# The second adaLN pass moved from attention to the paired merge-gate products, in halves of a block

## The chip, the cores and the metric

The kernel runs on one core of one Trainium2 chip. The metric is the device time of one execution in microseconds (us). Three runs of the kernel before took 3650.43, 3655.60 and 3663.57 us; the median is 3655.6 us. A measurement of this kernel can tell about 0.3% from no change.

## What is computed

The program is one step of a diffusion backbone of two layers over 128 prompt tokens and 1024 sample tokens, with a model width of 1024. In each layer adaLN makes a shift, a scale and a gate for every feature out of a conditioning vector, for the prompt and for the sample apart. The three go into the norm ahead of the layer and into the residual at its end. The gates `merge_g` of the merge are 3072 of the columns of the layer's input projection.

```python
def adaln_projection(x, cond, p):
    mod = jax.nn.silu(cond) @ p['w_ada'] + p['b_ada']
    shift, scale, gate = jnp.split(mod[:, None, :], 3, axis=-1)
    h = rms_norm(x, p['norm_g']) * (1.0 + scale) + shift
    return split_columns(h @ p['w_in']), gate

def merge_branches(o_a, o_b, o_c, merge_g, p):
    s_a, s_b, s_c = jnp.split(jax.nn.sigmoid(merge_g), N_BRANCH, axis=-1)
    m = s_a * (o_a @ p['w_pa']) + s_b * (o_b @ p['w_pb']) + s_c * (o_c @ p['w_pc'])
    return m @ p['w_o']

x = x + res_gate * merge_branches(o_a, o_b, o_c, merge_g, p)
```

`w_ada` has 1024 rows and 3072 columns in a layer. The kernel takes its columns in six blocks of 512: 0 and 1 are the shift, 2 and 3 the scale, 4 and 5 the gate.

## The kernel before

A layer runs in three parts: `front` (input projection, short convolutions, DeltaNet), `attention` and `mix` (merge gates, branch projections, merge, output projection, residual, next norm). Activations are held with features on the partitions. In the parts that use single-pass TensorE operands, a value is split into a rounded high part and a low part, and each product is three matmuls.

**Order.** In `front` and `mix` the code is written as streams (generators) that yield one instruction at a time. `Flow` (line 183) holds modelled costs and delays, and always emits the instruction that could start first by its model, with a small preference by rank (`RK`, line 264). Streams wait for each other by named events. All instructions that go through `Flow` have line 98 in the profile. `attn_all` (line 1241) emits directly, and its instructions have line 95. Each engine works off its own queue in that order.

**Attention.** `attn_all` goes through groups: a head and half of the sample tokens, nine blocks of keys each, a slot for each block, and two groups for the prompt at the end. In a slot `st` multiplies keys by queries (three matmuls), ACT takes the exponential into `P`, and POOL adds `P` up in `acc`. Three slots later the group's products with V follow (`po`), and the sums (`sm`). Twelve row maxima of the group after next are computed meanwhile: PE writes `s` into one of two places in PSUM (pool `pa`), and DVE reduces it to `mx` (`s1`, line 1311).

**adaLN.** Blocks 0 to 3 of layer 0 are computed at the start of the program (`s_ad`). The others are computed by `s_adv` (line 601) in attention: blocks 4 and 5 of layer 0 and 0 to 3 of layer 1 in layer 0, and blocks 4 and 5 of layer 1 in layer 1. For a block it loads eight tiles of 128 features by 512 columns (256 KB) in turn into two places. For each tile and each of the two conditioning vectors one instruction multiplies by a scalar of the partition and adds to an accumulator `ada` of 512 columns, on ACT for the first tile and on DVE for the rest. Then PE sums the accumulator over partitions with a matrix of ones (`adr`), ACT copies it (`ads`), PE turns rows into columns (`adc`), and DVE writes `mod` (`mod_put`, line 533). The table `AD` (line 767) spreads these steps evenly over the slots.

**Merge gates.** At the start of `mix` the stream `s_sg` (line 2113) computes the gates for three weight tiles directly, then for ten pairs of weight tiles with seven products in place of eight (a product is two halves of 288 tokens, 12 matmuls each). The order of the seven is in `SB`. `s_sh` (line 2006) makes the sums of activations, `s_sw` (line 2031) loads the weights of a pair (`ss`, `ws`), makes four sums of them on DVE, and splits each of the seven operands on ACT and POOL into its place (`sl0` to `sl4` and two in a tile `wh_sl`). `s_se` evicts each half product on DVE or ACT out of one of six places in PSUM, and `s_sx` takes tanh on ACT and stores the gates through SP. Event `sw{n}_{i}` says that operand i of pair n is in its place, `sp{n}_{i}` that its product has ended.

## Time and profile before

| what | value |
|---|---|
| median of 3 runs | 3655.6 us (3650.43 to 3663.57) |
| the profiled execution | 3672.03 us, its span 3670.1 us |
| busy: PE, DVE, POOL, ACT | 94%, 63%, 42%, 32% |
| attention with adaLN, layer 0 | 1006 to 1253 us, mean granted clock 0.78 |
| products of the pairs, layer 0 | 1397 to 1620 us, mean granted clock 1.00 |
| attention with adaLN, layer 1 | 2820 to 3039 us, mean granted clock 0.89 |

The profile shows one execution. Busy shares are means over stages with different limits, so a change in one stage is read from that stage. The granted clock is TensorE's, as a share of its full speed of 2.4 GHz; the other level is 1.2 GHz, and a mean between them says how long each held. Of the name in a row, the part to the left of the arrow is what an instruction writes and to the right what it reads. A matmul of plain 32-bit operands shows as two records.

### The profile page before, as it was taken

To read this page: it belongs to the slowest core of one execution; us is meant where nothing else is said; L and a number is where in the kernel's file an instruction comes from. 1 tells how busy PE (TensorE), PEld (TensorE's weight loads), DVE (VectorE), ACT (ScalarE), POOL (GpSimd) and SP (SyncE) were. 2 spreads that over 40 slices of the span, in tenths; PEclk is the share of its full clock that TensorE was granted. 3 is DMA by queue.
4 is the path that set the end of the run, shared out by engine and by line. 5 is a ranking of instruction groups with operands and counts; after the bars stand their busy time and mean duration, and the time that the engine had idled before them with its cause. 6 is when DMAs were issued, how large, how long until landed. Compare 5 with 4: busy or idle time off the path is not lost. (4 is left out here: it accounts for less than half of the span.)

```text
span 3670.1 us, 65225 instructions
## 1 busy us (share of the span) xinstructions
PE 3460.2 (94%) x24622; PEld 2934.9 (80%) x24622; DVE 2319.4 (63%) x4956; ACT 1189.8 (32%) x2543; POOL 1526.5 (42%) x1534
## 2 busy tenths in 40 slices
PE   7999999998978999999999999999998899999998
PEld 4988777778844589999999877777887557999998
DVE  4477676755577756447565777777456764743756
ACT  4432222224232333332344232122243333333234
POOL 3165556432244545422322645654313654542241
PEclk9999889999977899999999999999999989999999
DMA  5232212225633323347422233123265322333842
GB/s 185 93 109 74 58 49 74 69 57 167 192 92 97 76 69 99 105 130 240 147 100 92 88 79 80 46 55 81 82 202 154 89 56 62 99 99 115 252 148 84
DMA packets 372409, 389.62 MB, mean 106 GB/s; under 512 B 161280, under 2 KB 293056, under 8 KB 371712
## 3 DMA queue, kind: packets, MB, share of 16 engines
q1 hardware_dynamic: 372096, 385.46, 35.8%
q8 instruction: 195, 3.19, 0.4%
q14 instruction: 118, 0.97, 0.1%
HBM read 264.54 MB, written 120.72 MB: 105 GB/s over the span
## 5 line engine op out<-in xcount | busy, mean ns | idle before, releaser
L98 PE MATMUL ip<-h,wh_wi 128*128 128x384 f32 x5328 | 1165.2, 357 | 2.3 <-DVE gb L98 1.1
L98 PEld LDWEIGHTS ip<-h,wh_wi 128*128 128x128 f32 x5328 | 930.6, 194 | 55.3 <-issue 17.2
L95 POOL TENSOR_TENSOR acc<-acc,P 128x512 f32<-128x512 f32 x224 | 301.4, 1346 | 215.2 <-ACT P L95 203.9
L98 POOL TENSOR_TENSOR tmp<-M,X 128x2 f32<-128x2 f32 (+30 forms) x310 | 216.3, 698 | 278.1 <-DVE X L98 260.1
L95 DVE TENSOR_REDUCE mx<-s 128x1 f32<-128x384 f32 (+1 forms) x400 | 209.7, 542 | 183.3 <-PE s L95 177.1
L95 ACT ACTIVATE P<-st 128x512 f32<-128x512 f32 x292 | 173.6, 597 | 396.1 <-PE st L95 359.7
L95 PE MATMUL st<-q,K 97*128 97x512 f32 (+1 forms) x912 | 295.1, 440 | 0.0
L98 POOL TENSOR_TENSOR mU<-mU,mt 128x384 f32<-128x384 f32 x96 | 112.7, 1175 | 266.5 <-DVE mt L98 266.5
L95 PEld LDWEIGHTS st<-q,K 97*128 97x128 f32 x912 | 184.0, 214 | 42.7 <-issue 16.5
L98 POOL TENSOR_TENSOR wh_wi<-wri,wh_wi 128x512 fp32r<-128x512 f32 x112 | 153.1, 1377 | 156.0 <-ACT wh_wi L98 153.7
L98 PE MATMUL pp<-ob,wp 128*128 128x384 f32 x1152 | 210.4, 341 | 5.9 <-ACT ob L98 3.9
L98 PEld LDWEIGHTS pp<-ob,wp 128*128 128x128 f32 x1152 | 201.7, 190 | 14.0 <-ACT ob L98 6.9
L95 PE MATMUL s<-K,q 96*128 96x384 f32 (+1 forms) x400 | 150.3, 397 | 66.1 <-DVE mx L95 54.0
L98 POOL TENSOR_TENSOR sl<-ss,sl 128x512 fp32r<-128x512 f32 x100 | 140.0, 1403 | 155.4 <-ACT sl L98 143.7
L98 PE MATMUL wop<-h,wh_wo 128*128 128x384 f32 x1152 | 203.4, 336 | 0.5 <-DVE wh_wo L98 0.5
L98 DVE TENSOR_REDUCE X<-tmp 128x1 f32<-128x2 f32 (+30 forms) x620 | 184.6, 319 | 29.8 <-POOL tmp L98 22.0
L98 PEld LDWEIGHTS wop<-h,wh_wo 128*128 128x128 f32 x1152 | 199.6, 188 | 2.2 <-DVE wh_wo L98 1.1
L98 PE MATMUL sg<-T,sl 128*128 128x288 f32 x1440 | 194.4, 295 | 0.6 <-POOL sl L98 0.6
L98 PEld LDWEIGHTS sg<-T,sl 128*128 128x128 f32 x1440 | 192.0, 188 | 0.9 <-POOL sl L98 0.8
L98 ACT ACTIVATE VT<-pv,sst 128x64 f32<-128x64 f32 x256 | 66.4, 310 | 370.9 <-DVE scr L98 354.4
L95 PEld LDWEIGHTS s<-K,q 96*128 96x128 f32 x400 | 86.1, 215 | 119.9 <-DVE mx L95 91.5
L98 DVE TENSOR_TENSOR tmp<-M,X 128x2 f32<-128x2 f32 (+30 forms) x310 | 164.7, 531 | 19.4 <-POOL M L98 13.5
(343 smaller groups left out, 6376.5 us busy)
## 6 DMA issues: line engine op xcount, KB each, us to landing
wri<-in_w_in SPq DMA_DIRECT2D x160, 256.0 KB, 3.4
mt<-mD SPq DMA_DIRECT2D x144, 192.0 KB, 2.6
wada<-in_w_ada SPq DMA_DIRECT2D x64, 256.0 KB, 2.9
or<-oD SPq DMA_DIRECT2D x72, 192.0 KB, 3.6
wrp<-in_w_p SPq DMA_DIRECT2D x48, 256.0 KB, 3.6
mD<-C SPq DMA_DIRECT2D x80, 144.0 KB, 1.8
mD<-cu SPq DMA_DIRECT2D x80, 144.0 KB, 1.8
ss<-in_w_in SPq DMA_DIRECT2D x40, 256.0 KB, 3.6
```

The source lines that it names most:

```text
L95: return real(*a, **kw)
L98: op.f = lambda: real(*a, **kw)
```

## The change

`s_adv` becomes a stream of the first part of `mix`, with rank 4, and starts when the sums of activations have ended (`sT`). It works on half a block at a time: tiles of 128 features by 256 columns (128 KB) in two places, one accumulator of two times 256 columns. The sum over partitions is made by four matmuls for a half, with the accumulator as the stationary operand and one column of ones as the moving one, so that the result stands in columns at once; the matmuls with rows, their copy on ACT and the turning fall away. The rest of attention is the same.

Operand 3 of a pair takes the place of operand 0 (`slot[0]`), and `sl3` falls away. Its split is now the last of the pair and waits for product 0 of the same pair; the split of operand 0 waits for product 3 of the pair before. The accumulator's buffer serves `s_sh` as a scratch tile first.

```diff
--- before.py
+++ after.py
@@ -262,7 +262,7 @@
 
 
 RK = dict(ad=1, mk=0, mkb=5, xl=0, adl=1, w=2, ip=9, ev=1, cv=4, la=0, ga=7, gb=6, gv=4, gz=4, gc=3, gd=4, w2=2, lb=3, ln=0, ln1=1,
-          mw=2, mg=4, mp=5, em=1, ep=0, ob=3, xo=4, ms=1, mk1=3, ad1=4, adl1=1, mo=3, sh=3, sw=2, sg=5, se=0, sx=1)
+          mw=2, mg=4, mp=5, em=1, ep=0, ob=3, xo=4, ms=1, mk1=3, ad1=4, adl1=1, mo=3, sh=3, sw=2, sg=5, se=0, sx=1, adv=4)
 
 
 class Kern:
@@ -598,54 +598,43 @@
                 yield from cols
                 cols = None
 
-    def s_adv(self, blocks):
-
-
-        cs = yield from self.cond(blocks[0][0])
-        items = [(l, b, k) for l, b in blocks for k in range(KC)]
+    def s_adv(self, l):
+
+
+        yield Wait("sT")
+        cs = yield from self.cond(l)
+        blocks = [(l, b) for b in (4, 5)] + [(k, b) for k in range(l + 1, min(l + 2, L)) for b in range(4)]
+        items = [(k, b, x, kc) for k, b in blocks for x in range(2) for kc in range(KC)]
         w = {}
 
         def load(i):
             if i < len(items):
-                l, b, k = items[i]
-                w[i] = self.pt.tile([128, 512], F32, tag="wad", bufs=2, name=f"wada{l}_{b}_{k}")
-                yield self.ld(w[i], self.A["w_ada"][l, b][:, k * 512:k * 512 + 512])
-
-        def sums(l, b, acc):
-            rows = self.PA(f"adr{l}_{b}")
+                k, b, x, kc = items[i]
+                w[i] = self.al(self.pt, [128, 256], F32, "wad", 2, f"wada{k}_{b}_{x}_{kc}")
+                yield self.ld(w[i], self.A["w_ada"][k, b][:, kc * 512 + x * 256:kc * 512 + x * 256 + 256])
+
+        yield from load(0)
+        for i, (k, b, x, kc) in enumerate(items):
+            yield from load(i + 1)
+            if kc == 0:
+                if b == 0 and x == 0:
+                    self.mod_tiles(k)
+                acc = self.al(self.pt, [128, self.HC], F32, "wac", 1, f"ada{k}_{b}_{x}")[:, 0:512].rearrange("p (c x) -> p c x", c=2)
             for c in range(2):
-                yield self.mm(rows[c * 32:c * 32 + 32, :], self.ones[:, 0:32], acc[:, c], tile_position=(0, c * 32))
-            sr = self.pt.tile([128, 512], F32, tag="sr", name=f"ads{l}_{b}")
-            yield self.cp("a", sr[0:64], rows[0:64])
-            yield
-            yield
-            ps = self.PA(f"adc{l}_{b}")
-            for i in range(4):
-                yield self.mm(ps[:, i * 2:i * 2 + 2], sr[0:64, i * 128:i * 128 + 128], self.ident[0:64, 0:33:32])
-            yield from self.mod_put(l, b, ps)
-
-        for i in range(2):
-            yield from load(i)
-        todo = iter(())
-        for i, (l, b, k) in enumerate(items):
-            if k == 0:
-                if b == 0:
-                    self.mod_tiles(l)
-                acc = self.pt.tile([128, 2, 512], F32, tag="wah", bufs=2, name=f"ada{l}_{b}")
-            for c in range(2):
-                s = cs[:, k, c:c + 1]
-                if k == 0:
+                s = cs[:, kc, c:c + 1]
+                if kc == 0:
                     yield self.nc.scalar.activation(out=acc[:, c], in_=w[i], func=AF.Copy, scale=s)
                 else:
                     yield self.stt(acc[:, c], w[i], s, acc[:, c], ALU.mult, ALU.add)
-            yield from load(i + 2)
-
-            if k:
-                next(todo, None)
-                next(todo, None)
-            if k == KC - 1:
-                todo = sums(l, b, acc)
-        yield from todo
+            if kc == KC - 1:
+                if x == 0:
+                    ps = self.al(self.ppa, [128, 512], F32, "pa", 2, f"adc{k}_{b}")
+                for j in range(2):
+                    for c in range(2):
+                        o = (2 * x + j) * 2 + c
+                        yield self.mm(ps[:, o:o + 1], acc[:, c, j * 128:j * 128 + 128], self.ones[:, 0:1])
+                if x:
+                    yield from self.mod_put(k, b, ps)
 
 
     def rstd(self, acc, n, nm, buf, psum, res=None):
...
-    AD = (14, 24)
...
-        ad = [(l, b) for b in (4, 5)] + [(k, b) for k in range(l + 1, min(l + 2, L)) for b in range(4)]
-        ga = self.s_adv(ad)
-        n0, n1, m = *self.AD, len(ad) * 31 + 12
-        for i in range(m):
-            add(n0 + i * (NS - n1 - n0) // m, next, ga, None)
-        add(NS - n1 + 1, lambda: self.now(ga))
...
@@ -1971,7 +1950,8 @@
         R = lambda S: {n: dict(rank=RK[n], gen=g) for n, g in S.items()}
         X = {}
         with self.pool("pS", 1) as self.pt, self.pool("ppS", 1, space=PSUM) as self.ppm:
-            S = R(dict(sh=self.s_sh(l, X), sw=self.s_sw(l, X), sg=self.s_sg(l, X), se=self.s_se(l, X), sx=self.s_sx(l, X)))
+            S = R(dict(sh=self.s_sh(l, X), sw=self.s_sw(l, X), sg=self.s_sg(l, X), se=self.s_se(l, X), sx=self.s_sx(l, X),
+                       adv=self.s_adv(l)))
             fl.run(S)
         with self.pool("pm", 1) as self.pt, self.pool("ppm", 1, space=PSUM) as self.ppm:
             X["o"] = {}
@@ -2012,7 +1992,8 @@
 
         cf = cu.rearrange("p a x -> p (a x)")
         a, b = cf[:, N1], cf[:, N2]
-        c, e = (self.pt.tile([128, 1024], F32, tag=f"sl{i}", name=f"tq{l}_{i}")[:, N1] for i in (3, 4))
+        c = self.pt.tile([128, 1024], F32, tag="sl4", name=f"tq{l}")[:, N1]
+        e = self.al(self.pt, [128, self.HC], F32, "wac", 1, f"te{l}")
         for k in range(4):
             whole = lambda g, o, k, n: self.tt(g, o, f(h[:, k, 0, n]), f(h[:, k, 1, n]), ALU.add)
             yield whole("v", a, k, N2)
@@ -2033,7 +2014,9 @@
 
         def place(n):
             for i in range(len(slot), n):
-                slot.append(self.pt.tile([128, 1024], F32R, tag=f"sl{i}", name=f"sl{l}_{i}").rearrange("p (s x) -> p s x", s=2))
+
+                slot.append(slot[0] if i == 3 else self.pt.tile([128, 1024], F32R, tag=f"sl{i}", name=f"sl{l}_{i}").rearrange(
+                    "p (s x) -> p s x", s=2))
 
         place(3)
         tile_ = lambda x: self.A["w_in"][l, MT_MG + self.BR[x // 8] * 8 + x % 8]
@@ -2056,7 +2039,7 @@
             def free(i):
 
                 if not first:
-                    yield Wait(f"sp{n - 1}_{i}")
+                    yield Wait(f"sp{n - 1}_{3 if i == 0 else i}")
 
             yield self.ld(a11, w1[:, 0:512])
             r1, r2 = (self.al(self.pev, [128, 512], F32, "wr", 2, f"ws{l}_{n}_{x}") for x in range(2))
@@ -2079,9 +2062,6 @@
             yield from free(2)
             yield from split(2, s2)
             yield Set(f"sw{n}_2")
-            yield from free(3)
-            yield from split(3, s1)
-            yield Set(f"sw{n}_3")
             yield from free(4)
             yield from split(4, a11)
             yield Set(f"sw{n}_4")
@@ -2095,6 +2075,9 @@
             yield from free(6)
             yield from split(6, r2)
             yield Set(f"sw{n}_6")
+            yield Wait(f"sp{n}_0")
+            yield from split(3, s1)
+            yield Set(f"sw{n}_3")
         X["w"] = {}
         X["w"][23] = self.wh(f"mg{l}_23")
         yield from self.split_w(X["w"][23], 1024, tile_(23), f"m{l}_23", "p")
```

In DVE's queue in attention of layer 0 the maxima `mx` of group 4 stand between sums of adaLN (`ada`) before:

```order
L95 TENSOR_SCALAR nm_3_10601<-mx_3_10232 128x4
L95 TENSOR_REDUCE mx_4_10466<-s_4_0_10603 128x1
L95 TENSOR_REDUCE mx_4_10466<-s_4_1_10606 128x1
L95 SCALAR_TENSOR_TENSOR ada_4_10567<-wada_4_2_10580,cs_10547,ada_4_10567 128x512
L95 TENSOR_REDUCE mx_4_10466<-s_4_2_10624 128x1
L95 TENSOR_REDUCE mx_4_10466<-s_4_3_10639 128x1
L95 SCALAR_TENSOR_TENSOR ada_4_10567<-wada_4_3_10613,cs_10547,ada_4_10567 128x512
L95 RECIPROCAL sm_0_10505<-sm_0_10505 128x256
L95 TENSOR_REDUCE mx_4_10466<-s_4_4_10669 128x1
```

and now:

```order
L95 TENSOR_SCALAR nm_3_10588<-mx_3_10232 128x4
L95 TENSOR_REDUCE mx_4_10466<-s_4_0_10590 128x1
L95 TENSOR_REDUCE mx_4_10466<-s_4_1_10593 128x1
L95 TENSOR_REDUCE mx_4_10466<-s_4_2_10608 128x1
L95 TENSOR_REDUCE mx_4_10466<-s_4_3_10622 128x1
L95 RECIPROCAL sm_0_10505<-sm_0_10505 128x256
L95 TENSOR_REDUCE mx_4_10466<-s_4_4_10649 128x1
```

The sums between the maxima are gone.

In DVE's queue at the products of pair 2 of layer 0 stood the evictions (`cu`, `C`, from the products `sg_pair_operand_half`) and the weight sums `ss` of the pair to come:

```order
L98 TENSOR_TENSOR cu_13002<-sg_1_6_1_13578,cu_13002 128x288
L98 TENSOR_TENSOR C_2_0_13658<-sg_2_1_0_13633,cu_13002 128x288
L98 TENSOR_TENSOR C_2_1_13666<-sg_2_1_1_13648,cu_13002 128x288
L98 TENSOR_TENSOR ss_13229<-ws_3_0_13608,ws_3_1_13609 128x512
L98 TENSOR_TENSOR ss_13229<-ss_13229 128x512
L98 TENSOR_TENSOR cu_13002<-sg_2_2_0_13665,cu_13002 128x288
L98 TENSOR_TENSOR cu_13002<-sg_2_2_1_13686,cu_13002 128x288
L98 TENSOR_TENSOR cu_13002<-sg_2_3_0_13701,cu_13002 128x288
```

Now the sums of the second half of block 4 stand there, two for each load `wada`, and the weight sums come later:

```order
L98 TENSOR_TENSOR cu_12731<-sg_1_6_1_13357,cu_12731 128x288
L98 SCALAR_TENSOR_TENSOR ada_4_1_13279<-wada_4_1_3_13347,cs_13056,ada_4_1_13279 128x256 x2
L98 SCALAR_TENSOR_TENSOR ada_4_1_13279<-wada_4_1_4_13360,cs_13056,ada_4_1_13279 128x256 x2
L98 SCALAR_TENSOR_TENSOR ada_4_1_13279<-wada_4_1_5_13394,cs_13056,ada_4_1_13279 128x256 x2
L98 SCALAR_TENSOR_TENSOR ada_4_1_13279<-wada_4_1_6_13406,cs_13056,ada_4_1_13279 128x256 x2
L98 TENSOR_TENSOR C_2_0_13457<-sg_2_1_0_13416,cu_12731 128x288
L98 TENSOR_TENSOR C_2_1_13463<-sg_2_1_1_13440,cu_12731 128x288
L98 TENSOR_TENSOR cu_12731<-sg_2_2_0_13462,cu_12731 128x288
L98 TENSOR_TENSOR cu_12731<-sg_2_2_1_13481,cu_12731 128x288
L98 SCALAR_TENSOR_TENSOR ada_4_1_13279<-wada_4_1_7_13443,cs_13056,ada_4_1_13279 128x256 x2
L98 TENSOR_TENSOR cu_12731<-sg_2_3_0_13495,cu_12731 128x288
L98 SCALAR_TENSOR_TENSOR mod_158<-adc_4_13265,sm_122 128x8
```

Four loads' sums lie between the last eviction of pair 1 and the first one of pair 2 on DVE, and the last load's directly behind the eviction of half 2_2_1.

In PE's queue at the same place the products followed one another:

```order
L98 MATMUL sg_2_1_1_13648<-h,sl_1_12996 128x288 x12
L98 MATMUL sg_2_2_0_13665<-T_1_12999,sl_2_12997 128x288 x12
L98 MATMUL sg_2_2_1_13686<-T_1_12999,sl_2_12997 128x288 x12
L98 MATMUL sg_2_3_0_13701<-T_0_12998,sl_3_13327 128x288 x12
L98 MATMUL sg_2_3_1_13719<-T_0_12998,sl_3_13327 128x288 x12
```

and now the sums over partitions (`adc`) stand among them:

```order
L98 MATMUL sg_2_1_1_13440<-h,sl_1_12725 128x288 x12
L98 MATMUL sg_2_2_0_13462<-T_1_12728,sl_2_12726 128x288 x12
L98 MATMUL sg_2_2_1_13481<-T_1_12728,sl_2_12726 128x288 x12
L98 MATMUL sg_2_3_0_13495<-T_0_12727,sl_0_12724 128x288 x10
L98 MATMUL adc_4_13265<-cst,ada_4_1_13279 128x1
L98 MATMUL sg_2_3_0_13495<-T_0_12727,sl_0_12724 128x288 x2
L98 MATMUL sg_2_3_1_13513<-T_0_12727,sl_0_12724 128x288
L98 MATMUL adc_4_13265<-cst,ada_4_1_13279 128x1 x3
L98 MATMUL sg_2_3_1_13513<-T_0_12727,sl_0_12724 128x288 x11
```

The first of four `adc` has moved in ahead of the last two matmuls of half 2_3_0, and the other three behind the first matmul of half 2_3_1; operand 3 comes from `sl_0`.

In POOL's queue the splits of pair 2 stood in the order of the products:

```order
L98 TENSOR_TENSOR sl_0_12995<-ss_13229,sl_0_12995 128x512
L98 TENSOR_TENSOR sl_1_12996<-ss_13229,sl_1_12996 128x512
L98 TENSOR_TENSOR sl_2_12997<-ss_13229,sl_2_12997 128x512
L98 TENSOR_TENSOR sl_3_13327<-ss_13229,sl_3_13327 128x512
L98 TENSOR_TENSOR sl_4_13328<-ss_13229,sl_4_13328 128x512
L98 TENSOR_TENSOR wh_sl_13364<-ss_13229,wh_sl_13364 128x512
L98 TENSOR_TENSOR wh_sl_13364<-ws_2_1_13395,wh_sl_13364 128x512
```

and now:

```order
L98 TENSOR_TENSOR sl_1_12725<-ss_12958,sl_1_12725 128x512
L98 TENSOR_TENSOR sl_2_12726<-ss_12958,sl_2_12726 128x512
L98 TENSOR_TENSOR sl_4_13057<-ss_12958,sl_4_13057 128x512
L98 TENSOR_TENSOR wh_sl_13086<-ss_12958,wh_sl_13086 128x512
L98 TENSOR_TENSOR wh_sl_13086<-ws_2_1_13144,wh_sl_13086 128x512
L98 TENSOR_TENSOR sl_0_12724<-ss_12958,sl_0_12724 128x512 x2
```

The split of operand 3 has moved behind that of operand 6 and goes to `sl_0`, where it stands with that of operand 0 of the next pair.

## Rows read from the trace of the kernel before

**Rows 1.** The page: busy us, share of the span, instructions; clock in 40 slices.
```profile
PE 3460.2 (94%) x24622; PEld 2934.9 (80%) x24622; DVE 2319.4 (63%) x4956; ACT 1189.8 (32%) x2543; POOL 1526.5 (42%) x1534
...
PEclk9999889999977899999999999999999989999999
```

**Rows 2.** Busy time by stretch: length, then engines in us (instructions), clock, DMA.
```profile
core 0: us, PE busy (x) PEld busy (x) DVE busy (x) ACT busy (x) POOL busy (x), PEclk, DMA share, GB/s
1006.21:1252.89 246.68, 205.01 (x683) 116.55 (x682) 190.15 (x276) 72.33 (x132) 111.00 (x82) 0.78 0.40 95
1252.89:1281.10 28.21, 27.70 (x124) 17.02 (x123) 19.01 (x36) 12.18 (x23) 19.53 (x16) 1.00 0.26 56
1396.90:1619.85 222.95, 222.87 (x1682) 222.64 (x1681) 101.88 (x181) 83.20 (x173) 96.35 (x72) 1.00 0.32 99
2820.11:3039.28 219.17, 198.74 (x757) 117.28 (x756) 152.42 (x251) 78.02 (x141) 130.19 (x97) 0.89 0.34 76
```

**Rows 3.** PE's timeline, attention of layer 0: start, us, operation [idle before <-releaser].
```profile
1006.21 4.08 PE L95 MATMUL po<-P,V 128*64 128x512 f32 x17
...
1038.60 0.69 PE L95 MATMUL s<-K,q 96*128 96x384 f32 x1 [3.80 <-DVE mx L95]
...
1059.18 1.92 PE L95 MATMUL adr<-ada,cst 128*32 128x512 f32 x4 [4.11 <-DVE mx L95]
...
1252.89 4.08 PE L95 MATMUL po<-P,V 128*64 128x512 f32 x17
...
1266.99 4.08 PE L95 MATMUL po<-P,V 128*64 128x512 f32 x17
...
1281.10 4.08 PE L95 MATMUL po<-P,V 128*64 128x512 f32 x17
```

**Rows 4.** PE's timeline, attention of layer 1.
```profile
2820.11 4.08 PE L95 MATMUL po<-P,V 128*64 128x512 f32 x17
...
3025.22 4.08 PE L95 MATMUL po<-P,V 128*64 128x512 f32 x17
...
3039.28 4.08 PE L95 MATMUL po<-P,V 128*64 128x512 f32 x17
```

**Rows 5.** Waits, 1006 to 1253 us: waiting engine <- releaser, us, times, longest.
```profile
PEld s L95 <- DVE mx L95: 44.8, 40, 4.1
...
PE s L95 <- DVE mx L95: 30.2, 21, 3.8
```

**Rows 6.** Sums of adaLN: count, ns min/median/max, first and last start, shapes.
```profile
L95 DVE SCALAR_TENSOR_TENSOR ada<-wada,cs,ada x112: 734/1283/1826, 1018.3 to 2977.2; 128x512 f32<-128x512 f32 x112
```

**Rows 7.** PE's timeline: three matmuls (six records) with one moving column.
```profile
1828.58 0.72 PE L98 MATMUL rs_h<-cst,ssa 128*128 128x1 f32 x6
1829.16 2.85 PE L98 MATMUL wop<-h,wh_wo 128*128 128x384 f32 x15
```

**Rows 8.** PE's timeline in a pair of merge-gate tiles; 12 matmuls are half a product.
```profile
1514.91 9.70 PE L98 MATMUL sg<-T,sl 128*128 128x288 f32 x72
1524.45 3.34 PE L98 MATMUL sg<-h,wh_sl 128*128 128x288 f32 x24
```

**Rows 9.** Weight sums, splits and evictions of the pairs: count, ns min/median/max.
```profile
L98 ACT ACTIVATE sl<-ss x100: 614/632/636, 1385.7 to 3349.2; 128x512 fp32r<-128x512 f32 x100
L98 POOL TENSOR_TENSOR sl<-ss,sl x100: 1280/1297/1830, 1387.1 to 3349.9; 128x512 fp32r<-128x512 f32 x100
...
L98 DVE TENSOR_TENSOR ss<-ss x40: 677/1668/1930, 1396.0 to 3344.0; 128x512 f32<-128x512 f32 x40
...
L98 DVE TENSOR_TENSOR cu<-sg,cu x200: 439/450/459, 1406.2 to 3377.9; 128x288 f32<-128x288 f32 x100
```

**Rows 10.** DMA issues: count, KB each, median us to landing.
```profile
wada<-in_w_ada SPq DMA_DIRECT2D x64, 256.0 KB, 2.9
...
ss<-in_w_in SPq DMA_DIRECT2D x40, 256.0 KB, 3.6
...
wr<-in_w_uk SPq DMA_DIRECT2D x8, 128.0 KB, 2.6
```

## The prediction

> **What bounds the kernel now.** I read the page first: PE is busy 94% of the span, and its clock row shows full speed nearly everywhere [rows 1]. So time is to be had only where PE waits or where its clock is down. The next view is busy time by stretch [rows 2]. The reader is to see three kinds of stretch there. In the attention of layer 0, while the sums of adaLN run (1006 to 1253 us), PE is busy 205 of 247 us, its mean granted clock is 0.78 and DVE is busy 190 us. In the same attention after the sums have ended (1253 to 1281 us), PE is busy 27.7 of 28.2 us, the clock is 1.00 and DVE is busy only 67%. In the stretch of the paired merge-gate products (1397 to 1620 us) PE is busy all the time at clock 1.00 and DVE only 102 of 223 us. Layer 1 shows the same with fewer sums: 0.89 in its attention.
>
> The third view is PE's timeline. I take the first product with V of a group of attention (`po`) as the mark of the group. Without adaLN the marks are 14.1 us apart: 1252.89, 1266.99, 1281.10 [rows 3], and 3025.22 to 3039.28 in layer 1 [rows 4]. With adaLN PE stands still for 3.80 and 4.11 us at a time for the row maxima of DVE (`mx`), and the matmul behind such a wait takes longer [rows 3]. The waits view names the same: 44.8 us before weight loads of `s` and 30.2 us before its matmuls, all released by DVE `mx` [rows 5]. One sum of adaLN over 512 columns takes DVE 0.73 to 1.83 us, 1.28 in the middle [rows 6], and two stand between two maxima, while `s` has two places in PSUM. So DVE is late, PE waits, and the idle time costs clock too.
>
> **What the change takes out of attention.** In layer 0 ten groups lie between the marks 1006.21 and 1252.89: 246.7 us against 10 x 14.1 = 141.0, a gain of 105.7 us. In layer 1 twelve groups lie between 2820.11 and 3039.28: 219.2 against 12 x 14.1 = 169.2, a gain of 50.0 us. These differences hold everything that adaLN did there: the DVE sums, 64 loads, PE's row and column sums, and the half clock. Sum 155.7 us. It is an upper bound as far as the clean groups are clean; I see no reason for less, since the clean groups still load q and K and compute the maxima of two groups on. What is late next there is PE itself: 27.7 of 28.2 us.
>
> **What it adds beside the products.** Eight blocks (six in layer 0, two in layer 1) become 16 halves. Each half has 8 loads of 128 KB, 14 sums on DVE of 256 columns, 2 scaled copies on ACT, and 4 matmuls on PE whose moving operand is one column. There is room for DVE, ACT and SP; PE has none, so each PE instruction counts in full.
>
> PE: the same form of matmul stands in the trace as the first step of a norm, three of them (six records) from 1828.58 to 1829.16, where the next product starts: 0.58 / 3 = 0.19 us [rows 7]. 64 x 0.19 = 12.4 us. The PE time that they had in attention is in the 155.7 already.
>
> Waits of PE for those sums: this the trace of before doesn't show. The order puts the first matmul of a half behind ten or so products of an eviction that DVE also waits for, and the last two sums right behind that eviction. Half a product (12 matmuls) takes 9.54 / 6 = 1.59 us [rows 8]. Walk it in pair 2: the eviction starts when six halves are done, at 9.54 + 0.2, and takes 0.45 [rows 9]; the two sums, which I take at 0.45 each (an estimate between half of 0.734 [rows 6] and the 0.45 of an eviction of 288 columns [rows 9]), end at 10.65 and 11.1; PE comes to the first matmul at 6.83 x 1.59 = 10.9. It just fits when DVE is not held up. It is held up when a split on POOL runs at the same time: the weight sums `ss<-ss`, from SBUF alone, take 0.68 us or 1.67, one POOL operation of 1.30 longer or nearly so [rows 9], while evictions from PSUM stay at 0.45. POOL has seven splits of 1.30 us in a pair of 22.3 us, 41%. So a wait of 0 to 1.3 us per half, I take 0.8: 16 x 0.8 = 12.8 us.
>
> The bound above that is the chain of loads. Two tiles take turns, so two items cost one load from issue to landing, one issue and one item of sums. 128 KB landed in 2.6 us in another busy stretch, 256 KB of the weights of this very stretch in 3.6 [rows 10]. With 0.4 for issue and 0.9 to 1.3 for the sums, eight items take 4 x 3.9 = 15.6 to 4 x 5.3 = 21.2 us, and 1.5 for handing over the single accumulator: 17.1 to 22.7. In layer 0 the sums of the first half end in the order after nine of the 140 half products and those of the twelfth after the last, so a half has 131 / 11 x 1.59 = 18.9 us of PE and 0.8 of its own matmuls: 19.7. Wait 0 to 3.0 us, so 0 to 48 us over 16 halves. I stay at 0.8, since the loads of the weights come in bursts of four and are away for most of a pair.
>
> Behind a sum that waits for its load on DVE stand evictions; PE feels them after six places in PSUM, 9.5 us. DVE's own load: 102 us of 223 now [rows 2], for a half 8.6 of 18.9 us with the start, and 14 x 0.45 = 6.3 more, and at most all of POOL's 7.7 us as lock: 22.6 against 19.7. This bound too is some 3 us per half.
>
> The Trainium skill ("Trainium Architecture — The Big Picture", What this means for kernel authors) says that DVE and GpSimd contend for one shared port pair as an exclusive lock and not as a split of bandwidth. It speaks against moving sums beside the splits; 0.68 against 1.67 agrees with it. By that rule in full, every split would hold DVE for its whole length, and the sum would be 16 x 2.9 = 46 us of waits in place of 12.8, a time of about 3558.
>
> **The shared place.** Operand 3 of a pair now has the place of operand 0, so its split waits until product 0 has ended, 3.2 us into the pair. ACT 0.63 and POOL 1.30 to 1.83 [rows 9] with 0.4 of hand-over end at 5.5 to 6.1; product 3 starts at 6 x 1.59 = 9.5. Behind the waiting copy on ACT stand the gates' tanh, whose eviction is not there before 4.97. Operand 0 of the next pair waits for product 3, ends at 12.7 + 2.4 and has until 22.3. Taken at nothing; the cover is 3.4 us. On SP the loads of halves stand ahead of the gates' stores and of the next weights; these have some 7 us. The sums that now share DVE with the first pair's set-up I leave at 0.
>
> **Sum.** 155.7 - 12.4 - 12.8 = 130.5 us. The profiled execution took 3672.0 us, so it would take 3541.5; the median of the runs is 16 us lower, 3655.6, and I take the same gain from it: 3525.
>
> **Rivals.**
> (1) The chain of loads or the lock bounds the halves: 48 us of waits in place of 12.8, 3655.6 - 155.7 + 12.4 + 48 = 3560. For it: the bursts at 3.6 us. Against it: DVE is under half busy.
> (2) The shared place has no cover: with ACT or POOL late by 2 us at product 3 of 20 pairs, 40 us: 3565. Against it: the 3.4 us above.
> (3) Attention doesn't come down to 14.1: if the loads of q and K need the slower pace and groups stay at 18 us, 22 x 3.9 = 86 us are missing: 3611. Against it: the clean groups.
> (4) The other side: the two tiles don't overlap. If SP holds each load behind stores that wait for a tanh, or DVE takes up each item only after the next wait, an item costs 0.4 + 2.6 + 1.0 = 4.0 us, a half 32, so 16 x (32 - 19.7) = 197 us: 3655.6 - 155.7 + 12.4 + 197 = 3709, slower. It decides from 28.7 us per half, 3.6 per item. For it: SP keeps its order, and the sums stand in order among evictions. Against it: the next load stands ahead of the sums of this item.
>
> **How the numbers follow.** Chances: forecast 0.74, (1) 0.10, (2) 0.07, (3) 0.05, (4) 0.04. With no waits at all it is 3655.6 - 155.7 + 12.4 = 3512, and the runs shown spread 5 us down and 8 up; (1) and (2) end at 3565 and 8. Range 3505 to 3573; (3), (4) and the worst of (1) and (2) lie outside. The bound for no change, about what a measurement here can tell, is 0.3%, 11 us. Faster: all but (4) and a mixture of (3) with waits: 0.94; same 0.02; slower 0.04.
>
> **What would show it.** Right: marks 14.1 us apart through both attentions at clock 1.00, no `mx` wait over 1.1 us; the stretch of the products 15 to 30 us longer in layer 0 and 4 to 10 in layer 1, the additional idle time of PE before the one-column matmuls. Rival 1: waits of 3 us there and clock below 1.00. Rival 2: PE idle before product 3, released by POOL. Rival 3: marks above 15 us. Rival 4: DVE idle for loads, each half 28 us or more. I am wrong if the clock or the evictions fall behind in the product stretch, so that PE waits for PSUM rather than for a sum.

## The result and the profile after

The changed kernel takes 3599.35 us (median of 4 runs, 3588.94 to 3608.03), the kernel before 3659.59 beside it (median of 4). The ratio is 0.984, 95% interval 0.980 to 0.987: faster by 60 us, well beyond the 0.3% that a measurement of this kernel can tell from no change. The forecast was 3525 us and a gain of 130; its range ended at 3573. The direction was right, the size was not, and the time lies outside the range.

The profiled execution has a span of 3606.1 us (3670.1 before). Its page, busy time and granted clock in 40 slices, answers to [rows 1]:

```profile
PE 3405.2 (94%) x24654; PEld 2925.5 (81%) x24654; DVE 2319.9 (64%) x5068; ACT 1190.1 (33%) x2551; POOL 1517.0 (42%) x1534
...
PEclk9999899999999999999999999999999999999999
```

The dip to 7 in attention is gone. Busy time by stretch answers to [rows 2]: length, engines, PEclk, DMA share and GB/s. The lines are attention of layer 0 (eleven groups), the pairs of layer 0, attention of layer 1 (twelve groups), the pairs of layer 1.

```profile
1002.39:1160.71 158.32, 154.17 (x672) 93.75 (x671) 105.98 (x201) 68.18 (x125) 113.84 (x89) 0.99 0.34 74
1289.57:1572.75 283.18, 254.44 (x1778) 249.94 (x1777) 202.67 (x358) 94.35 (x200) 100.83 (x72) 0.93 0.39 124
2779.18:2949.91 170.73, 166.48 (x733) 101.88 (x733) 115.52 (x219) 74.34 (x136) 124.15 (x97) 1.00 0.33 72
3064.65:3312.26 247.61, 235.52 (x1714) 234.12 (x1713) 133.09 (x242) 87.78 (x183) 95.88 (x72) 0.97 0.33 106
```

Attention did what was forecast: ten groups from 1002.39 to 1146.64 take 144.3 us in place of 246.7, twelve in layer 1 take 170.7 in place of 219.2. That is 150.9 us (102.4 and 48.5). PE's timeline shows the last marks of layer 0 14.1 us apart, which answers to [rows 3]; in the mean they are 14.4 us apart in layer 0 and 14.2 in layer 1, since waits for `mx` of 4.1 and 4.2 us are left, the longest 1.25:

```profile
1146.64 4.08 PE L95 MATMUL po<-P,V 128*64 128x512 f32 x17
...
1160.71 4.08 PE L95 MATMUL po<-P,V 128*64 128x512 f32 x17
...
1174.82 1.51 PE L95 MATMUL po<-P,V 128*64 128x512 f32 x6
```

The pairs gave more than half of it back. In layer 0 they take 283.2 us (223.0 before), in layer 1 247.6 (225.2): 82.6 us where the forecast had 25.2. PE, which was busy for 222.87 of 222.95 us in layer 0, now stands still for 28.7 us, and it is busy for 31.6 us longer at a mean clock of 0.93. Its waits there (engine and what it waited before, releaser, us, times, longest):

```profile
PE adc L98 <- DVE ada L98: 24.2, 16, 5.1
PE sg L98 <- ACT sl L98: 2.8, 1, 2.8
PE sg L98 <- POOL sl L98: 1.6, 1, 1.6
```

In layer 1 the waits for sums come to 7.7 us:

```profile
PE adc L98 <- DVE ada L98: 7.7, 4, 3.3
```

`adc` is the one-column matmuls. PE's timeline shows one such wait in layer 0; [rows 8] have the same matmuls at full speed, 72 records in 9.54 us:

```profile
1363.52 0.38 PE L98 MATMUL adc<-cst,ada 128*128 128x1 f32 x2 [1.16 <-DVE ada L98]
1363.77 0.65 PE L98 MATMUL sg<-T,sl 128*128 128x288 f32 x3
1364.25 0.72 PE L98 MATMUL adc<-cst,ada 128*128 128x1 f32 x6
1364.84 9.61 PE L98 MATMUL sg<-T,sl 128*128 128x288 f32 x59
```

The last 59 matmuls take 9.44 us to the next start (1374.28), nearly as long as 72 at full speed. Busy time by stretch shows when the clock was down, for this wait and for a longer one:

```profile
1363.52:1364.84 1.32, 1.32 (x12) 1.32 (x12) 0.80 (x2) 0.00 (x0) 0.00 (x0) 1.00 0.91 268
1366.00:1368.00 2.00, 2.00 (x11) 2.00 (x10) 0.46 (x1) 0.41 (x1) 0.00 (x0) 0.50 0.87 304
1370.00:1372.00 2.00, 2.00 (x17) 2.00 (x16) 1.55 (x5) 0.79 (x2) 0.08 (x1) 1.00 0.22 54
...
1465.71:1475.00 9.29, 9.29 (x71) 9.29 (x72) 3.69 (x8) 3.45 (x9) 2.58 (x2) 1.00 0.72 231
```

PE stood for 1.16 us until 1363.52. Right behind the wait the clock is still 1.00; from 1366 to 1368, when PE is busy all the time, it is 0.50 (1.2 GHz), and from 1370 it is 1.00 again. Not every wait is followed by a drop: behind one of 2.56 us that ends at 1465.71 the clock stays at 1.00.

Why are the sums late? DVE's and POOL's timelines of the next half, DVE first:

```profile
1369.60 0.88 DVE L98 SCALAR_TENSOR_TENSOR ada<-wada,cs,ada 128x256 f32<-128x256 f32 x2 [2.13 <-DMA wada<-in_w_ada]
...
1371.67 1.91 DVE L98 SCALAR_TENSOR_TENSOR ada<-wada,cs,ada 128x256 f32<-128x256 f32 x2
...
1378.48 2.59 DVE L98 SCALAR_TENSOR_TENSOR ada<-wada,cs,ada 128x256 f32<-128x256 f32 x2
```

```profile
1371.92 2.82 POOL L98 TENSOR_TENSOR sl<-ss,sl 128x512 fp32r<-128x512 f32 x2 [11.64 <-ACT sl L98]
1378.07 2.72 POOL L98 TENSOR_TENSOR sl<-ss,sl 128x512 fp32r<-128x512 f32 x2 [3.33 <-ACT sl L98]
```

Two sums take 0.88 us when POOL is idle, and 1.91 or 2.59 while POOL does two splits in a row. Counted in the trace over both layers, the 119 sums during which POOL does nothing take 0.47 to 0.49 us each, and the 105 that overlap an operation of POOL take 1.05 us in the mean. The planner (`Flow`) reckons 0.40 for one. Over the stage of layer 0 the 168 sums take 0.74 us in the mean, and DVE stands for 31.3 us before their loads (this row: busy us, mean ns, then the idle time before them and its releasers):

```profile
L98 DVE SCALAR_TENSOR_TENSOR ada<-wada,cs,ada 128x256 f32<-128x256 f32 x168 | 117.7, 740 | 34.2 <-DMA wada<-in_w_ada 31.3 <-ACT ada L98 2.3
```

SP's queue, which issues these loads in order with the weights' loads and the gates' stores, stood for 74.5 us before loads whose tile DVE still read:

```profile
SPq L98 <- DVE ada L98: 74.5, 55, 3.7
SPq L98 <- ACT C L98: 33.6, 32, 4.3
```

So two suspects stand in the trace, the late loads and the long sums, and a third in the order: the matmuls come right behind the last sum.

### The profile page after: what moved, and what is told of

Same layout as the page of the kernel before. It is cut to its first block, busy times and chain, and to the rows that moved or that the text cites. A ratio compares the mean times of both kernels' runs of the same rounds, so it can differ in the third digit from the quotient of the medians.

```text
span 3606.1 us, 65480 instructions
## 1 busy us (share of the span) xinstructions
PE 3405.2 (94%) x24654; PEld 2925.5 (81%) x24654; DVE 2319.9 (64%) x5068; ACT 1190.1 (33%) x2551; POOL 1517.0 (42%) x1534
## 5 line engine op out<-in xcount | busy, mean ns | idle before, releaser
L95 POOL TENSOR_TENSOR acc<-acc,P 128x512 f32<-128x512 f32 x224 | 289.4, 1292 | 127.4 <-ACT P L95 111.2
L95 PE MATMUL st<-q,K 97*128 97x512 f32 (+1 forms) x912 | 257.0, 393 | 0.0
L98 PE MATMUL sg<-T,sl 128*128 128x288 f32 x1440 | 211.4, 307 | 8.8 <-ACT sl L98 5.5
L98 POOL TENSOR_TENSOR wh_wi<-wri,wh_wi 128x512 fp32r<-128x512 f32 x112 | 152.2, 1370 | 158.8 <-ACT wh_wi L98 156.7
L98 PEld LDWEIGHTS sg<-T,sl 128*128 128x128 f32 x1440 | 204.8, 199 | 9.7 <-ACT sl L98 6.0
L98 DVE SCALAR_TENSOR_TENSOR ada<-wada,cs,ada 128x256 f32<-128x256 f32 x224 | 158.0, 746 | 45.1 <-DMA wada<-in_w_ada 40.7
L95 PEld LDWEIGHTS st<-q,K 97*128 97x128 f32 x912 | 163.9, 190 | 28.4 <-issue 11.5
L98 POOL TENSOR_TENSOR gm<-g,cst 128x256 fp32r<-128x256 f32 x144 | 107.8, 760 | 163.9 <-PE sg L98 126.1
```

What stands on the lines that cost most here:

```text
L95: return real(*a, **kw)
L98: op.f = lambda: real(*a, **kw)
```

## The experiments

The part of the program ahead of attention is alike in all of them, and yet the first product with V stands between 989.6 and 1018.6 us in the profiles. Totals carry this scatter, so the lengths of the two stages (from the first product of the pairs to the start of the direct products of the last weight tile) are compared first; each is read from one profile. All numbers of the table are from the views of busy time by stretch and of waits; the waits are PE's before the one-column matmuls. The runs were made in three sets, each with its own runs of the kernel before (medians 3659.8, 3664.6 and 3665.1 us, by the order of the sections); the ratios are to those, and a difference of times across sets carries some 5 us.

| kernel | layer 0, us (clock) | layer 1, us (clock) | waits for sums, us | time, us | ratio to before, interval |
|---|---|---|---|---|---|
| before | 223.0 (1.00) | 225.2 (1.00) | none | 3659.6 | |
| after | 283.2 (0.93) | 247.6 (0.97) | 24.2, 7.7 | 3599.4 | 0.984, 0.980 to 0.987 |
| no sums | 225.5 (1.00) | 225.5 (1.00) | none | 3514.2 | 0.961, 0.959 to 0.962 |
| before, place only | 224.5 (1.00) | 228.5 (0.99) | none | 3667.4 | 1.002, 1.000 to 1.005 |
| no wait for sums | 261.6 (0.98) | 237.8 (0.98) | none | 3578.5 | 0.978, 0.974 to 0.981 |
| no wait for loads | 261.3 (0.97) | 234.2 (0.99) | 12.4, 0.9 | 3562.5 | 0.974, 0.971 to 0.977 |
| neither wait | 240.9 (0.99) | 232.5 (0.99) | none | 3544.7 | 0.966, 0.961 to 0.970 |
| short splits | 246.6 (0.99) | 240.7 (0.98) | 4.4, 4.5 | 3565.6 | 0.971, 0.967 to 0.976 |
| third tile | 283.8 (0.93) | 250.9 (0.96) | 29.3, 12.3 | 3596.7 | 0.981, 0.976 to 0.986 |
| third tile and slack | 252.1 (0.97) | 238.0 (0.98) | 7.2, 3.0 | 3553.1 | 0.969, 0.965 to 0.973 |
| slack for matmuls, two tiles | 279.2 (0.93) | 243.1 (0.96) | 23.8, 4.9 | 3588.1 | 0.979, 0.976 to 0.982 |
| slack for matmuls, three tiles | 268.4 (0.95) | 242.6 (0.97) | 18.8, 6.2 | 3578.1 | 0.977, 0.973 to 0.980 |
| third tile, slack, two pieces | 245.9 (0.99) | 234.3 (0.99) | 4.5, 3.0 | 3542.5 | 0.966, 0.963 to 0.969 |
| the same, more slack | 241.5 (0.99) | 234.0 (0.99) | 2.7, 2.0 | 3544.2 | 0.966, 0.963 to 0.969 |

### No sums

```
-        cs = yield from self.cond(l)
-        blocks = [(l, b) for b in (4, 5)] + [(k, b) for k in range(l + 1, min(l + 2, L)) for b in range(4)]
...
+        mod = self.lay[l]["mod"]
+        yield self.nc.vector.memset(mod[:, 16:24, :], 0.25)
+        yield self.nc.vector.memset(self.lay[l]["gt"], 0.125)
...
```

> The changed kernel with all of adaLN's sums taken out of the paired stage (their loads, sums, copies and one-column matmuls are left out; the modulation is constants); the shared place of operands 0 and 3 stays. Theory: attention really gives back about 151 us, and what is lost is lost beside the products. The two paired stages, 283.2 and 247.6 us in the changed kernel, come to 223 to 228 and 225 to 230 us, and the time to about 3510 us (3505 to 3520 with 0 to 5 us per layer for the shared place in the first pair). Rival: the sums are not what makes the paired stages longer but the shared place: they stay above 245 and 240 us, 3545 us or more. Rival: attention gives back less than its marks say: above 3530 us with paired stages of 225 us.

Measured: 3514.22 us, stages of 225.5 and 225.5 us at clock 1.00. Busy time by stretch:

```profile
1278.21:1503.74 225.53, 223.07 (x1682) 222.68 (x1681) 94.36 (x186) 84.50 (x175) 92.80 (x72) 1.00 0.31 98
...
2991.70:3217.24 225.54, 223.08 (x1682) 222.69 (x1682) 94.30 (x184) 84.50 (x175) 92.81 (x72) 1.00 0.31 98
```

The theory holds. Attention's gain is real, the shared place costs 2.5 us of idle time in the first pair of a layer, and the sums lengthen the stages by 57.7 and 22.1 us.

### The shared place alone

```
-                slot.append(self.pt.tile([128, 1024], F32R, tag=f"sl{i}", name=f"sl{l}_{i}").rearrange("p (s x) -> p s x", s=2))
+                slot.append(slot[0] if i == 3 else self.pt.tile([128, 1024], F32R, tag=f"sl{i}", name=f"sl{l}_{i}").rearrange(
+                    "p (s x) -> p s x", s=2))
...
-            yield from free(3)
-            yield from split(3, s1)
...
+            yield Wait(f"sp{n}_0")
+            yield from split(3, s1)
```

> The kernel before with one part of the change alone: operand 3 of a pair in the place of operand 0, split after product 0; adaLN stays in attention. Theory: only the first pair has no cover, where the changed kernel's PE waits 2.8 and 1.6 us for the two halves of operand 3; so 0 to 5 us per layer, 3660 to 3670 us. Rival (shared place without cover in every pair): 40 us, 3700 us.

Measured: 3667.42 us, 0 to 0.5% slower; the stages are 1.5 and 3.3 us longer. In layer 1 PE waits, as in the kernel after, before products of the first pair alone:

```profile
PE sg L98 <- ACT sl L98: 2.3, 1, 2.3
PE sg L98 <- POOL sl L98: 1.4, 2, 0.8
```

Of the 1.4 us, 0.6 stand in the kernel before as well. So the cover holds in eighteen pairs; in the first pair of a layer it doesn't.

### No wait for the sums

The planner still reckons with the accumulator (`op.r`), so the order stays. PE no longer reads the accumulator, so the next half needn't wait for PE before it writes there either.

```
-   yield self.mm(ps[:, o:o + 1], acc[:, c, j * 128:j * 128 + 128], self.ones[:, 0:1])
+   op = self.mm(ps[:, o:o + 1], self.ident, self.ones[:, 0:1])
+   a = acc[:, c, j * 128:j * 128 + 128]
+   op.r.append((self.key(a), _span(a)))
+   yield op
```

> The changed kernel, instruction by instruction in the same order, but the one-column matmuls read the resident identity instead of the accumulator of the sums, so PE never waits for a sum (the column sums of the products with the features are left out). Theory (the waits cost twice, as idle time and as half clock behind them): the paired stages come down to about 223 + 9 + 4 = 236 and 225 + 3 + 4 = 232 us, the granted clock there to 0.99 or more, the time to about 3538 us (3530 to 3550). Rival (DVE's load and the lock delay the evictions, and PE only waits elsewhere): PE's waits move to places in PSUM, the paired stages stay above 262 and 240 us, the time above 3570 us.

Measured: 3578.51 us, 261.6 and 237.8 us. My theory fell. The waits for sums were 24.2 us and are gone, but the stage of layer 0 still has 19.2 us of idle time, put down to other releasers. Waits of PE, then of DVE, in that stage:

```profile
PE sg L98 <- POOL sl L98: 6.5, 7, 1.6
PE sg L98 <- ACT sl L98: 5.3, 4, 2.8
PE mg L98 <- DVE cu L98: 3.3, 1, 3.3
PE sg L98 <- DVE cu L98: 3.0, 5, 1.2
...
DVE ada L98 <- DMA wada<-in_w_ada: 56.8, 42, 5.2
```

When PE no longer waits for the sums, DVE waits longer for their loads (56.8 us in place of 31.3), and behind it stand the evictions and the weight sums from which splits are made. The rival nearly had the stages (262 and 240 us) and had the time; only it named the evictions as the first to be late, and of PE's waits 11.8 us are for splits (4.4 of them, in the first pair, stand in the kernel after too) and 6.3 for evictions.

### No wait for the loads

```
...
-   yield self.stt(acc[:, c], w[i], s, acc[:, c], ALU.mult, ALU.add)
+   op = self.stt(acc[:, c], self.two, s, acc[:, c], ALU.mult, ALU.add)
+   op.r.append((self.key(w[i]), _span(w[i])))
+   yield op
```

> The changed kernel in the same order, but the sums and their first copies read two resident tiles of constants instead of the loaded tile; all loads are still issued, nobody waits for them (the data of the loads are left out of the sums). Theory A (late loads make the sums late): PE's waits for sums fall from about 24 and 8 us in the two paired stages to under 8 and 3, the clock there to 0.98 or more, the time to 3545 to 3560 us. Theory B (the sums themselves are slow beside POOL, and the hand-over of the single accumulator): the waits stay above 16 and 5 us, the time is 3580 us or more.

Measured: 3562.5 us, 37 us less than after. The result lies between the theories, in time nearer to A. In layer 1 the waits go from 7.7 to 0.9 us as A has it, in layer 0 half of them stays:

```profile
PE adc L98 <- DVE ada L98: 12.4, 11, 2.6
```

The sums still take 0.75 us in the mean, so it is not the loaded tile that makes them long.

### Neither wait

Both edits together.

> The changed kernel in the same order, with both edits of the two runs before together: the sums read resident constants (all loads are still issued, nobody waits for them) and the one-column matmuls read the resident identity (the data of the loads and of the sums are left out). Theory (two separate causes, late loads on DVE's queue and matmuls placed too close behind the sums, are together all of it): the paired stages come to 225.5 + 9.1 + 2 = 237 and 225.5 + 3.0 + 2 = 231 us at clock 0.99 or more, the time to 3530 to 3545 us. Rival (the sums' length beside POOL, or DVE's load, delays the evictions by itself): the stages stay above 250 and 236 us, PE waits for places in PSUM, 3555 us or more.

Measured: 3544.69 us. Busy time by stretch:

```profile
1275.07:1515.94 240.87, 236.46 (x1777) 236.00 (x1777) 207.13 (x357) 92.48 (x200) 102.59 (x72) 0.99 0.47 145
...
3001.77:3234.25 232.48, 228.10 (x1713) 227.64 (x1713) 134.23 (x242) 87.66 (x183) 97.08 (x72) 0.99 0.36 113
```

The theory holds, with stages 4 and 1 us above it. DVE is busier than in the kernel after (207.1 us against 202.7), with sums of 0.78 us in the mean, and PE waits for nothing but the splits of the first pair: DVE's load is not the limit. The two layers also give the price of the one-column matmuls: PE is busy for 13.4 us more than without sums for 48 of them and 5.0 more for 16, so 8.4 / 32 = 0.26 us each and 0.8 us per layer besides.

### Short splits

```
-            yield self.lo(g, slot[i][:, 1], src, slot[i][:, 0])
+            full = self.lo(g, slot[i][:, 1], src, slot[i][:, 0])
+            op = full if n == self.SP[0] else self.lo(g, slot[i][:, 1, 0:64], src[:, 0:64], slot[i][:, 0, 0:64])
+            op.r, op.w, op.c = full.r, full.w, full.c
+            yield op
```

> The changed kernel in the same order, but from the second pair of each layer on POOL's subtractions of the splits do 64 of 512 columns (the rest of the operands' low parts is left out), so POOL holds the port an eighth as long. Theory (the lock has a small share, loads and places the larger): the sums fall to 0.47 to 0.5 us each, but DVE still waits some 25 us or more for loads in the first paired stage and PE 15 us or more for sums; the gain is under 15 us, 3585 to 3599 us. Rival (the lock is the main cause): PE's waits fall under 8 us, the stages below 250 and 236 us, the time to 3560 us or less.

Measured: 3565.63 us, 34 us less than after. My theory had the sums and DVE's waits right and fell on PE: the stage of layer 0 comes down by 36.6 us. The row of the sums there, and PE's waits for them:

```profile
L98 DVE SCALAR_TENSOR_TENSOR ada<-wada,cs,ada 128x256 f32<-128x256 f32 x168 | 77.8, 503 | 34.9 <-DMA wada<-in_w_ada 28.9 <-ACT sl L98 3.4 <-ACT ada L98 2.3
```

```profile
PE adc L98 <- DVE ada L98: 4.4, 3, 2.2
```

A sum takes 0.50 us in place of 0.74, and DVE waits for the loads as long as before (28.9 us); yet PE's waits for sums fall from 24.2 to 4.4 us. So POOL's splits are the larger cause in layer 0. In layer 1 the rival's 236 us were not reached (240.7, waits 4.5 of 7.7 us). Evictions, whose first operand is in PSUM, stayed at 0.45 us with long splits or short ones. The Trainium skill ("SBUF — State Buffer", SBUF: two separate sides) states just this: the shared ports are locked for a whole instruction between GpSimd and, among others, DVE operations that have two SBUF inputs. The trace agrees on both kinds of operation, the sums (0.74 us, and 0.50 with short splits) and the evictions (0.45 both times).

### A third tile

```
-   w[i] = self.al(self.pt, [128, 256], F32, "wad", 2, f"wada{k}_{b}_{x}_{kc}")
+   w[i] = X["big"][:, 512 + i % 3 * 256:768 + i % 3 * 256]
...
-   yield from load(i + 1)
+   yield from load(i + 2)
...
```

The accumulator and the three places lie in one tile `big`, and the table `gt` has one buffer in place of two.

> The changed kernel with a third tile for the loads of the sums (each load is issued two items ahead instead of one; the room comes from tiles that share a place), all else by the same planner. Theory: DVE's waits for these loads fall from 31 us to under 12 in the first paired stage, PE's waits for sums to about the 12.4 us that were left when nobody waited for loads, as the matmuls stand as close behind the sums as before: stages of 255 to 265 and 232 to 238 us, 3560 to 3570 us. Rival (the loads are late because of their place in SP's queue and the bursts of the weights, however early they are allowed): DVE waits 25 us or more, 3585 us or more.

Measured: 3596.69 us, the same as after within what can be told. The theory had DVE's waits for loads (4.6 us) and not PE's: PE waited longer than before. The waits of PE, then of DVE, in layer 0:

```profile
PE adc L98 <- DVE big L98: 29.3, 9, 7.8
...
DVE big L98 <- DMA big<-in_w_ada: 4.6, 2, 4.2
```

The planner, which reckons 0.40 us for a sum, uses earlier loads to pack the halves closer: in its order the twelfth half ends after 1358 of the 1680 product matmuls of layer 0, and in the kernel after behind the last. PE's one-column matmuls again stand right behind sums that take twice as long as planned. Earlier data alone gains nothing here as long as the planner sets the matmuls by its own time for a sum.

### A third tile and slack

```
-        return t
+        return t + op.d
...
+                op.d = 0.6 if c == 0 else 0.0
...
+                        op.d = 2.0 if j == 0 and c == 0 else 0.0
```

An item is one loaded tile with its two sums.

> As the run with the third tile, and the planner also reckons 2.0 us more before the one-column matmuls of a half and 0.6 us more for each item of the sums to be ready, so that both stand later in the order. Theory (both causes removed, only the matmuls' own 9.1 and 3.0 us and the first pair's 2.5 stay): stages of 235 to 242 and 229 to 232 us at clock 0.99 or more, PE's waits for sums under 5 us, the time 3530 to 3545 us, faster than the changed kernel by 55 to 70 us. Rival (what is taken from PE's waits for sums comes back as late evictions): 3570 us or more, with PE waiting for places in PSUM.

Measured: 3553.14 us, 46 us less than after and 8 above the expected range; the times expected for the stages were 10 and 6 us too short, the clock is 0.97 and 0.98. PE's waits for sums fell to 7.2 us in 7 times, and none of the rival's late evictions shows:

```profile
PE adc L99 <- DVE big L99: 7.2, 7, 2.1
PE sg L99 <- POOL sl L99: 1.7, 1, 1.7
PE sg L99 <- ACT sl L99: 1.0, 1, 1.0
```

### Slack for the matmuls alone, with two tiles and with three

The edit of the run before with 2.0 us before the matmuls and 0 for the items, first on the kernel after, then with the third tile.

> The changed kernel with two tiles as before, and the planner reckons 2.0 us more before the one-column matmuls of a half, nothing else. With the run of the third tile (no slack) and the run of both it makes a table of two by two. Theory (the sums are late because POOL's port lock stretches them past the planner's 0.40 us, and the matmuls stand right behind the last sum; the tiles only set how much slack fits): PE's waits for sums in the first paired stage fall from 24 to about 10 us, the stages to 262 to 270 and 238 to 242 us, the time to 3570 to 3585 us. Rival (the loads are the cause, slack only shifts the wait): waits stay above 18 us, 3590 us or more.

> The third tile, and the planner reckons 2.0 us more before the one-column matmuls of a half, but nothing more for the items of the sums. Theory: the matmuls' slack carries most of the gain of the run that has both (3553 us); without the items' 0.6 us DVE stands a little longer before loads: stages of 252 to 260 and 238 to 241 us, 3553 to 3565 us. Rival (the 0.6 us per item, which spreads the sums over the stage, carries it): PE's waits for sums above 15 us, stages above 268 and 244 us, 3575 us or more.

Measured: 3588.08 and 3578.07 us. With two tiles the rival's waits came (23.8 us) and nearly its time (3588 against 3590), for another reason: the slack makes the twelve halves longer than the stage, and the last one stands behind the last product. That one wait is 11.3 us; the other eleven come to 12.5, near my theory's 10. PE's timeline:

```profile
1550.11 0.64 PE L99 MATMUL sg<-T,wh_sl 128*128 128x288 f32 x3
1562.08 1.87 PE L99 MATMUL adc<-cst,ada 128*128 128x1 f32 x8 [11.34 <-DVE ada L99]
```

With three tiles it fits, but 18.8 us of waits stay, as the rival had it, and its time came too (3578 against 3575); I had expected most of the gain here. The 0.6 us per item, which keep the planner from packing the sums, bring 16.3 of the 31.7 us by which the run with both shortens layer 0. In layer 1, where four halves have a whole stage, slack gives 4.5 us with two tiles.

### POOL's subtractions in two pieces

```
-            yield self.lo(g, slot[i][:, 1], src, slot[i][:, 0])
+            for x in (slice(0, 256), slice(256, 512)):
+                yield self.lo(g, slot[i][:, 1, x], src[:, x], slot[i][:, 0, x])
```

The third tile and slack stay. In the second run the slack is 3.0 us for the matmuls and 0.3 for an item.

> As the run with the third tile, 2.0 us and 0.6 us of slack (3553 us), and POOL's subtraction of a split comes in two pieces of 256 columns instead of one of 512, so that it holds the port for half as long at a time. Theory (a sum waits for the POOL instruction that runs): the longest sum falls from 1.58 us to about 1.0, PE's waits for sums from 7.2 to under 4 us in the first paired stage, the stages to 245 to 250 and 234 to 237 us, the time to 3538 to 3550 us. Rival (DVE gets its turn no sooner, since POOL starts its second piece at once): the longest sum stays at 1.3 us or more, the time 3550 us or more.

> As the run with POOL's subtractions in two pieces, with 3.0 us of slack before the one-column matmuls and 0.3 us for each item of the sums instead of 2.0 and 0.6. Theory (what is left of PE's waits is slack that is too short, not DVE's load): waits for sums under 2 us, stages of 243 to 247 and 233 to 236 us, near the 240.9 and 232.5 us of the run in which nothing waits for sums or loads; 3535 to 3545 us. Rival: DVE's load is the limit, and the time stays within 5 us of the run with 2.0 and 0.6.

Measured: 3542.47 and 3544.18 us, 55 to 57 us below the kernel after and 121 to 123 below the kernel before. The row of the sums in layer 0 of the first run, and busy time by stretch of the second:

```profile
L99 DVE SCALAR_TENSOR_TENSOR big<-big,cs 128x256 f32<-128x256 f32 x168 | 102.8, 653 | 15.9 <-DMA big<-in_w_ada 12.0 <-ACT big L99 3.9
```

```profile
1294.23:1535.76 241.53, 236.22 (x1778) 235.17 (x1777) 189.09 (x359) 92.55 (x199) 119.38 (x140) 0.99 0.46 144
```

The mean sum of the first run falls from 0.72 to 0.65 us, though POOL is busy for 18 us longer. Its longest sum is 1.48 us, above the rival's 1.3, but not beside a split in two pieces. DVE's and POOL's timelines:

```profile
1511.99 1.48 DVE L99 SCALAR_TENSOR_TENSOR big<-big,cs 128x256 f32<-128x256 f32 x1
```

```profile
1511.90 1.28 POOL L99 TENSOR_TENSOR wh_mg<-wrm,wh_mg 128x512 fp32r<-128x512 f32 x1 [2.17 <-ACT wh_mg L99]
```

It stands beside an operation for the last weight tile (`wh_mg`) that the edit leaves whole, at 512 columns. Beside pieces of 256 columns no sum of that run takes more than 1.03 us, and the longest sum of the second run takes 1.00 (min/median/max in ns):

```profile
L99 DVE SCALAR_TENSOR_TENSOR big<-big,cs x224: 468/592/1003, 1303.6 to 3094.4; 128x256 f32<-128x256 f32 x112
```

So the first theory's longest sum of about 1.0 us came where the pieces are, and its rival, that DVE gets its turn no sooner, falls. The first run's time is in its expected range, its waits for sums in layer 0 (4.5 us) are a little above. With more slack the time stays within 2 us of the first run, as the second rival had it, though not for its reason, DVE's load: the stage of layer 0 falls by 4.4 to 241.5 us, 0.7 above the run in which nothing waits. Of the kernels that leave nothing out these two are the fastest.

## Why the prediction failed, by its own steps

**Attention: right.** 155.7 us forecast, 150.9 measured, marks 14.4 and 14.2 us apart in the mean, clock 0.99 to 1.00. One wait for `mx`, of 1.25 us, is above the bound of 1.1. (The reading that two sums stand between two maxima holds for 20 of the 64 places between 1010 and 1245 us that have any; in 44 it is one. No number hangs on it.)

**The one-column matmuls: too cheap.** 64 x 0.19 = 12.4 us were forecast from [rows 7]; between the products they cost 0.26 each, 16.8 us.

**The waits for sums: the step that failed.** The walk through pair 2 took a sum at 0.45 us beside a lock that comes now and then, and put 0.8 us on a half. The waits are 24.2 and 7.7 us, 31.9 in all, 2.0 per half. Both ways in which the prediction let a half wait were set too low, the lock and the loads. Of the lock the trace had the price: [rows 9] show SBUF-only operations of DVE at 0.68 or 1.67, and I gave it a share of 41% of one POOL operation, while splits come two and three in a row and the planner puts PE where a sum of 0.40 us would end. The short splits took 19.8 of the 24.2 us away. For the loads the prediction's own bound was 0 to 3.0 us per half, and it stayed at 0.8 because the weights' bursts are away for most of a pair; DVE stood for 31.3 us before its loads in layer 0, and without that wait 12.4 of the 24.2 us are left. The rule of the Trainium skill ("Trainium Architecture — The Big Picture", What this means for kernel authors) that the prediction weighed, the exclusive lock, came to 46 us of waits and 3558. The 31.9 us measured lie nearer to that than to my 12.8, and the short splits bear the lock out.

**The clock behind the waits: left out.** The sum has only idle time. In layer 0 PE's busy time of 254.4 us stands against 236.5 when nothing waits, in layer 1 235.5 against 228.1: 25.4 us of matmuls at the lower clock, 0.8 us for each us waited in the mean over 20 waits. The same loss stood in attention [rows 2, 3], and I counted it there as a gain and not here as a cost.

**The shared place: not quite nothing.** The cover of 3.4 us is there from the second pair on. The first pairs and what they do to the clock make up 8.5 us (2.6 and 0.4 without sums, 5.5 more with them, from the runs without sums and without waits).

Together: 16.8 + 31.9 + 25.4 + 8.5 = 82.6 us, the measured growth of the two stages, against 25.2. Of the 66.5 us that the profiled gain falls short (64.0 against 130.5) these are 57.4, attention 4.8, and 4.3 are left as the net difference of the other stages, which no run here explains.

**The rivals.** The first one named the mechanism, and its sign came in the main (waits of up to 5.1 us, 2.0 per half in the mean against its 3, clock below 1.00). Its bounds of 3 us per half were large enough for the waits but held no clock, so 3560 and the range up to 3573 were too low. The second is excluded, the third too; the fourth didn't come, as a half takes 283.2 / 12 = 23.6 us, under the 28.7 from which it decides.

**What stays open.** The shares of loads and lock don't add up: in layer 0 the stage loses 42.3 us to both, 21.9 of them go with the loads' waits alone and 36.6 with short splits alone, perhaps since either delay by itself nearly fits the place, which is argued and not shown. In layer 1 it is 13.4 and 6.9 of 15.1. The sums with a place of its own for operand 3 were not tried, nor the slack of the items with two tiles.

## What to carry to other kernels

Where PE is full and at full speed, price a wait with the matmuls that run slowly behind it: here each us waited cost 0.8 us more in the mean. Where a planner sets the order, hold its cost of an instruction against the trace beside the work that it is moved to (0.40 reckoned, 0.74 measured), since a reader placed right behind a late result waited in every half here, and earlier data only let the planner pack closer. A third tile, slack in the order and shorter instructions on the engine that shares the ports together gave back some 55 us of what the move had lost.

## What had not been expected of the hardware

A sum of 128x256 from SBUF takes DVE 0.47 us at the least and up to 1.58 beside POOL (kernel after, duration min/median/max in ns):

```profile
L98 DVE SCALAR_TENSOR_TENSOR ada<-wada,cs,ada x224: 467/482/1580, 1299.1 to 3157.8; 128x256 f32<-128x256 f32 x112
```

Half of the sums take 0.48 us or less, so the mean of 0.74 comes from those beside POOL. The granted clock can fall after PE has gone back to work: behind the wait of 1.16 us that ended at 1363.52 it was 1.00 until 1364.84 and 0.50 from 1366 to 1368. A matmul with one moving column between other products costs PE 0.26 us. Splitting POOL's instruction in two made POOL busy for longer, 118.0 us in place of 100.3, and DVE for less, 189.0 in place of 200.2.
